# A two-layer GLA/NSA trunk: three weight chunks of layer 0 land in tiles of later tenants, the second output projection uses other banks, gates are written in place

## Chip, core and metric

The kernel runs on one core of a Trainium2 chip, as one program. The metric is the device time of one execution in microseconds (us). Five engines work in parallel, each through its own list of instructions in order: TensorE (PE, matmuls, with its weight loads as PEld), VectorE (DVE), ScalarE (ACT), GpSimd (POOL) and SyncE (SP), which issues nearly all loads here. They wait for one another by semaphores.

## What is computed

A trunk of two layers over 256 tokens of width 1024, all float32. Each layer is `x + rms_norm(mixer(rms_norm(x)))`. The mixer of layer 0 is chunked gated linear attention (GLA), that of layer 1 is native sparse attention (NSA). Cut to its core:

```python
def gla_mixer(h, w_in, w_gk_up, b_gk, head_norm, w_out):
    p = h @ w_in
    q, k, v, glr, z = jnp.split(p, [512, 1024, 2048, 2064], axis=-1)
    gk = jax.nn.log_sigmoid(glr @ w_gk_up + b_gk) / 16.0
    o = gla_chunked(heads(q, 128) * 128 ** -0.5, heads(k, 128), heads(v, 256), heads(gk, 128))
    o = rms_norm(o, head_norm)
    return (o * jax.nn.silu(z)) @ w_out

def nsa_mixer(h, ...):
    q, kc, vc, ks, vs, kw, vw, gl, z = jnp.split(h @ w_in, splits, axis=-1)
    # rope; compressed, selected and sliding-window softmax attention, gated by sigmoid(gl)
    return (gated_sum * jax.nn.silu(z)) @ w_out

def reference(x, ...):
    for i in range(2):
        h = rms_norm(x, pre_norm[i])
        y = gla_mixer(h, ...) if i == 0 else nsa_mixer(h, ...)
        x = x + rms_norm(y, post_norm[i])
    return x
```

## The kernel before

The 256 tokens are two tiles of 128, called t = 0 and t = 1. All products are made from split operands: a float32 value is written as hi (rounded by ACT's copy) plus lo (the rest, a subtraction on DVE or POOL), and `mm3` (L211 to L213) adds three matmuls, hi·hi, hi·lo and lo·hi, into one PSUM bank. `hT` is the normalized input, transposed and split.

Weights come in **chunks** of up to 512 columns. A `Chunk` has four units of 256 rows; `load` issues one DMA a unit from SP into a raw tile, `split_unit` makes two hi's on ACT (L190) and two lo's (L196) by a unit, on POOL or DVE by the table `LOS`. In layer 0 the chunks are, in order: r (the last columns of v and the decay's input glr), k, q, v0, v1 (344 columns each), z0, z1 (512 each), and then the two halves of the output weights. Chunks r, k and q have a written-out order on each engine (`split_in_line`, L434 and L438, with `line("act", ...)` and the like); the later ones are ordered by the tile scheduler, by explicit orders (`after`, `chain` for PE, `prev`) and by `paced`, which ties a split to a matmul of an earlier chunk. In layer 1 the chunks are kc, ks, kw, q, z and the output weights.

What is scarce sets the order of much of this:

- Raw tiles: four tiles of tag "raw" are shared by all chunks. A load waits until the lo's of the unit that had the tile before are done. SP's queue is in order, so a load that waits holds all behind it. One chunk, k, lands elsewhere: two units in `home`, a tile in the place that zT takes later, and one each in the places of "on" and "gpost", which also come later.
- PSUM banks: two of tag "acc", three "s", two "t", one "o". `proj` (v and the chunks of layer 1 with rows out) takes one "acc" bank for each t; `proj_T` (q and z, transposed) two. A bank is free when its evacuation is done: L517 on ACT and L518 on DVE for v, L363 for z, L618 for q, L269 on ACT and L276 on DVE for an output projection.
- The buffer of tag "of", a single one: it holds z (the bank times `rb`, the tokens' norm factors) while the tanh (L371, ACT) and the product (L372, DVE) make the gate in zT; `gated` (L356 to L358: DVE, ACT, DVE) uses the same tag.

Around the v chunks, `decay(t)` computes the log-sigmoid on ACT and DVE (L598 to L606), L633 multiplies it with a triangular matrix on PE, L636 and L637 take exponentials on ACT, and L644, L650, L661 and L662 scale q and k with them on DVE. `out_proj(t)` runs 16 steps of `mm3` over the 8 row blocks k and the two halves n of the output, the first four k first, since the gates of the second z chunk come late; then `residual` reads the banks (L269, L276), scales and adds to X (L281), and `pre_T` transposes the new X (L302 on PE) into hT of layer 1 (L307, L310, L311). That of t = 1 runs beside the first chunk of layer 1, kc, whose half for t = 0 needs only the tokens of t = 0.

The lines which set these places:

```python
o = [bank("s" if t == 0 else "acc") for _ in range(2)]            # out_proj
z = base.tile([P, 2, S], F32, tag="of", name=nm("z"))             # gate_of
ch_k = Chunk(w_in, G_K, 512).load(homes=[home[:, 0], home[:, 1], "on", "gpost"])
ch_v0 = Chunk(w_in, 1024, 344).load()
simple(ch_v0, lambda o, t: to_v(o, t, 0, 344), (ch_q, PA[1]), prev=queues["act"])
```

Of the kernel before, what the change touches and what calls it, by code (L numbers as in the profile page):

```python
# [16 lines left out]
P = 128  # L17
# [70 lines left out]
def hybrid_kernel(ctx: ExitStack, tc: tile.TileContext, x, positions, pre_norm, post_norm,  # L88
# [9 lines left out]
    def nm(s):  # L98
        _n[0] += 1
        return f"{s}_{_n[0]}"  # L100
# [54 lines left out]
    grow = lp.tile([2 * KT, P], F32, tag="grow", name="grow")  # L155
    nc.scalar.dma_start(X[:, 0, :H], xv[:, 0, :H])
    nc.scalar.dma_start(grow, pre_norm.rearrange("l (k p) -> (l k) p", p=P))
    dma(C0, cst[:, :C_L0])
    dma(X[:, 1, :H], xv[:, 1, :H])

# [179 lines left out]
    def out_proj(t, chunks, oT, gb):  # L340

        o = [bank("s" if t == 0 else "acc") for _ in range(2)]
        steps = [(k, n) for k in range(4) for n in range(2)] + [(k, n) for n in range(2) for k in range(4, KT)]
        done = residual(t, o, gb)
        for k, n in steps:
            a, b = mm3(o[n], [h[:, k, :] for h in oT[t]], chunks[n].part(k), k == 0, k == KT - 1)
            first = a if k == n == 0 else first
            if k == KT - 1:
                done(n)
        chain(first, b)  # L350

    def gated(bv, zt, hi, lo):

        of = base.tile([P, 4, P], F32, tag="of", name=nm("of"), bufs=1)
        of = of[:, :bv.shape[1], :]
        nc.vector.tensor_mul(of, bv, zt)  # L356
        nc.scalar.activation(hi, of, AF.Copy)
        return nc.vector.tensor_sub(lo, of, f(hi))  # L358

    def gate_of(o, dst):  # L360

        z = base.tile([P, 2, S], F32, tag="of", name=nm("z"))
        nc.vector.tensor_tensor(z, o.rearrange("p (j n) -> p j n", j=2), rb.unsqueeze(1).to_broadcast([P, 2, S]),  # L363
                                op=ALU.mult)
        silu2(z, dst)

    tanh = [None]

    def silu2(o, dst):

        tanh[0] = after(nc.scalar.activation(dst, o, AF.Tanh, scale=0.5), tanh[0])  # L371
        nc.vector.scalar_tensor_tensor(dst, dst, 1.0, o, op0=ALU.add, op1=ALU.mult)  # L372

# [7 lines left out]
    home = lp.tile([P, 2, 2, 512], F32, tag="zT", name="home")  # L381
    ch_k = Chunk(w_in, G_K, 512).load(homes=[home[:, 0], home[:, 1], "on", "gpost"])
    wraw = lp.tile([32, 512], F32, tag="E", name="wraw")
# [138 lines left out]
    def from_r(t):  # L522
# [12 lines left out]
        line("act", a)  # L535
        line("dve", b)
        glrs.append(glr)

    split_in_line(ch_k, 0)
# [3 lines left out]
    split_in_line(ch_k, 2)  # L543
    for t in range(NT):
        from_r(t)
    split_in_line(ch_k, 3)

# [9 lines left out]
    line("pool", nc.gpsimd.tensor_copy(wup[64:64 + n], f(wup[:n])))  # L557
    for u in range(4):
        split_in_line(ch_q, u)
# [55 lines left out]

    ch_v0 = Chunk(w_in, 1024, 344).load()
    for j, o in enumerate(proj_T(ch_q, hT, dict(zip(GM, (gates_T, lambda: decay(0), lambda: decay(1)))))):
# [4 lines left out]
    scale = float(np.float32(GDK ** -0.5))  # L622
    zT = lp.tile([P, KT, S], F32, tag="zT", name="zT")
    aTs, qees, kdds = [], [], []
# [52 lines left out]

    simple(ch_v0, lambda o, t: to_v(o, t, 0, 344), (ch_q, PA[1]), prev=queues["act"])
    ch_z = [Chunk(w_in, G_Z, 512).load()]
    simple(ch_v1, lambda o, t: to_v(o, t, 344, 688), (ch_v0, PA[2]))  # L680
    ch_z.append(Chunk(w_in, G_Z + 512, 512).load())
    gpost = row(post_norm, 0, D, lp, "gpost")

# [34 lines left out]
    for c in range(2):  # L718
        ch_z[c].split(((ch_v1, PA[3]), (ch_z[0], PA[4]))[c])
        for j, o in enumerate(proj_T(ch_z[c], hT)):  # L720
# [524 lines left out]
```

## Time and profile before

| | |
|---|---|
| median of 3 runs | 311.4 us (310.65 to 311.85) |
| the profiled execution | 312.61 us |
| its span in the profile | 310.5 us |
| granted TensorE clock, mean | 0.979 |
| busy: PE, DVE, ACT, POOL | 289.7, 217.3, 180.8, 167.7 us |
| DMA queue of SP | 43.96 MB, 45.2% of 16 engines' span |

A row of the timeline gives start and duration in us, the engine, the line of the kernel, the operation with the names of what it writes and reads, shapes, and a count where equal instructions that follow each other are joined; in brackets stands how long the engine was idle before it and what ended that. The list of waits groups such brackets. The granted clock is the share of its full rate that TensorE was given in a stretch. A stretch of PE's timeline tells more than its busy share over the span: at 93% it is one wait at a time that can still go.

### The profile page before, as it was taken

To read this page: it belongs to the slowest core of one execution; us is meant where nothing else is said; L and a number is where in the kernel's file an instruction comes from. 1 tells how busy PE (TensorE), PEld (TensorE's weight loads), DVE (VectorE), ACT (ScalarE), POOL (GpSimd) and SP (SyncE) were. 2 spreads that over 40 slices of the span, in tenths; PEclk is the share of its full clock that TensorE was granted. 3 is DMA by queue.
4 is the path that set the end of the run, shared out by engine and by line. 5 is a ranking of instruction groups with operands and counts; after the bars stand their busy time and mean duration, and the time that the engine had idled before them with its cause. 6 is when DMAs were issued, how large, how long until landed. Compare 5 with 4: busy or idle time off the path is not lost.

```text
span 310.5 us, 5351 instructions
## 1 busy us (share of the span) xinstructions
PE 289.7 (93%) x1788; PEld 242.3 (78%) x1788; DVE 217.3 (70%) x556; ACT 180.8 (58%) x468; POOL 167.7 (54%) x184
## 2 busy tenths in 40 slices
PE   6999989989999899499997999999999989999991
PEld 6888978989999688377895866789878877677551
DVE  0677847665888778766588452879997899696523
ACT  3786586878476259524453430657986569565211
POOL 1294719988449106652544512599758974533400
PEclk9999997999999999689999999999999999999998
DMA  7990504868737505485265568657602600010001
GB/s 226 395 309 1 155 30 129 256 204 268 241 103 229 179 0 153 146 199 183 76 179 167 155 251 271 218 162 235 201 2 72 199 1 2 2 69 0 2 0 68
DMA packets 28300, 44.56 MB, mean 144 GB/s; under 512 B 2865, under 2 KB 12513, under 8 KB 28274
## 3 DMA queue, kind: packets, MB, share of 16 engines
q1 hardware_dynamic: 28098, 43.96, 45.2%
q10 hardware_dynamic: 176, 0.27, 0.3%
q8 instruction: 14, 0.23, 0.3%
q14 instruction: 12, 0.10, 0.1%
HBM read 43.18 MB, written 1.05 MB: 142 GB/s over the span
## 4 chain that ended last, share of the span: by engine, by line
PE 61%; DVE 17%; issue 9%; DMA 4%; POOL 4%; ACT 3%; SPq 0%; POOLq 0%; DVEq 0%; ACTq 0%
PE acc L211 12%; PE acc L213 11%; PE acc L212 11%; DVE lo L196 6%; PE s L466 4%; PE o L1078 3%; PE o L884 3%; PE s L991 3%; DMA raw<-in_gla_w_in_dram 3%; PE t L1064 3%; PE s L211 3%; PE s L212 2%; PE s L213 2%; POOL lo L196 2%; DMA raw<-in_nsa_w_out_dram 1%
## 5 line engine op out<-in xcount | busy, mean ns | idle before, releaser
L196 POOL TENSOR_TENSOR lo<-raw,hi 128x512 fp32r<-128x512 f32 (+2 forms) x69 | 89.5, 1321 | 44.5 <-ACT hi L190 43.3
L190 ACT ACTIVATE hi<-raw 128x512 fp32r<-128x512 f32 (+2 forms) x128 | 68.2, 580 | 38.3 <-DMA raw<-in_nsa_w_in_dram 21.0
L196 DVE TENSOR_TENSOR lo<-raw,hi 128x512 fp32r<-128x512 f32 (+2 forms) x59 | 54.6, 946 | 19.0 <-ACT hi L190 18.9
L211 PE MATMUL acc<-hi,hT 128*128 128x512 f32 (+2 forms) x112 | 41.0, 366 | 5.1 <-DVE yg L276 4.0
L211 PE MATMUL acc<-hT,hi 128*128 128x256 f32 x160 | 45.1, 283 | 0.1
L213 PE MATMUL acc<-hT,lo 128*128 128x256 f32 x160 | 44.6, 282 | 0.0
L212 PE MATMUL acc<-hT,hi 128*128 128x256 f32 x160 | 44.5, 279 | 0.0
L1035 POOL TENSOR_SCALAR P<-P,cf 128x128 f32<-128x128 f32 (+1 forms) x64 | 29.9, 488 | 26.0 <-DVE cf L1031 14.3
L212 PE MATMUL acc<-lo,hT 128*128 128x512 f32 (+2 forms) x112 | 40.7, 363 | 1.0 <-POOL lo L196 0.7
L213 PE MATMUL acc<-hi,hT 128*128 128x512 f32 (+2 forms) x112 | 39.9, 356 | 0.0
L998 ACT ACTIVATE P<-P,mn 128x128 f32<-128x128 f32 (+1 forms) x64 | 28.4, 445 | 8.9 <-DVE mn L996 5.1
L211 PEld LDWEIGHTS acc<-hT,hi 128*128 128x128 f32 x160 | 30.0, 188 | 0.3 <-DVE z L363 0.3
L213 PEld LDWEIGHTS acc<-hT,lo 128*128 128x128 f32 x160 | 29.8, 188 | 0.5 <-issue 0.4
L212 PEld LDWEIGHTS acc<-hT,hi 128*128 128x128 f32 x160 | 30.1, 188 | 0.1
L211 PEld LDWEIGHTS acc<-hi,hT 128*128 128x128 f32 x112 | 22.0, 197 | 9.8 <-ACT hi L190 5.4
L212 PEld LDWEIGHTS acc<-lo,hT 128*128 128x128 f32 x112 | 22.0, 196 | 3.9 <-POOL lo L196 1.8
L996 DVE CUSTOM_DVE_ANT_0 P<-s,c 128x128 f32<-128x128 f32 (+1 forms) x64 | 20.7, 348 | 4.9 <-PE s L991 3.7
L213 PEld LDWEIGHTS acc<-hi,hT 128*128 128x128 f32 x112 | 22.0, 196 | 2.7 <-issue 0.4
L438 POOL TENSOR_TENSOR lo<-raw,hi 128x512 fp32r<-128x512 f32 (+1 forms) x9 | 11.6, 1302 | 14.7 <-ACT hi L434 14.7
L1064 PE MATMUL t<-c,P 128*128 128x128 f32 x96 | 16.6, 284 | 0.4 <-DVE qS L959 0.4
L275 POOL TENSOR_TENSOR ss<-ss,cols 128x1 f32<-128x1 f32 x4 | 2.2, 552 | 26.3 <-DVE ss L274 26.3
L822 POOL TENSOR_TENSOR dup<-rt,rt 128x512 f32<-128x512 f32 x6 | 8.6, 1438 | 13.4 <-DVE rt L815 11.3
(265 smaller groups left out, 675.0 us busy)
## 6 DMA issues: line engine op xcount, KB each, us to landing
raw<-in_nsa_w_in_dram SPq DMA_DIRECT2D x24, 512.0 KB, 4.5
raw<-in_gla_w_in_dram SPq DMA_DIRECT2D x14, 512.0 KB, 4.6
raw<-in_gla_w_out_dram SPq DMA_DIRECT2D x8, 512.0 KB, 5.0
raw<-in_nsa_w_out_dram SPq DMA_DIRECT2D x8, 512.0 KB, 4.3
raw<-in_gla_w_in_dram SPq DMA_DIRECT2D x8, 344.0 KB, 3.5
raw<-in_nsa_w_in_dram SPq DMA_DIRECT2D x8, 280.0 KB, 7.9
w<-in_nsa_ck_w_dram SPq DMA_DIRECT2D x4, 512.0 KB, 3.7
w<-in_nsa_cv_w_dram SPq DMA_DIRECT2D x4, 512.0 KB, 4.7
```

The costliest lines, as they stand in the source:

```text
L190: m = after(nc.scalar.activation(hi[:, j, :n], raw[:, j, :n], AF.Copy), prev)
L196: eng.tensor_sub(lo[:, j, :n], raw[:, j, :n], f(hi[:, j, :n]))
L211: m = nc.tensor.matmul(o, a[0], b[0], start=start, stop=False, **kw)
L212: nc.tensor.matmul(o, a[0], b[1], start=False, stop=False, **kw)
L213: return m, nc.tensor.matmul(o, a[1], b[0], start=False, stop=stop, **kw)
L438: line(e, eng.tensor_sub(lo[:, j, :n], raw[:, j, :n], f(hi[:, j, :n])))
L466: m = nc.tensor.matmul(o[t][:, :chunk.n], hT[i][:, k, t * P:(t + 1) * P], w[j], start=(k == b == 0), stop=(k == KT - 1 and b == 2))
L884: nc.tensor.matmul(hid_b[kv * 64:(kv + 1) * 64, :CHID], flat[:, j, kv].rearrange("p g c -> p (g c)"), w1[u * 2 + kv][:, j % 4, :], start=( ...
L996: nc.vector.tensor_tensor_reduce(out=o, in0=src, in1=masks[br], op0=ALU.add, op1=ALU.min, scale=-0.125, scalar=3.0e38, accum_out=self.mn[: ...
L998: nc.scalar.activation(o, o, AF.Exp, scale=-1.0, bias=self.mn[:, j:j + 1], accum_out=self.sm[:, j:j + 1])
L1035: nc.gpsimd.tensor_scalar(o, o, cf[:, i * 2 + br:i * 2 + br + 1], 1.0, op0=ALU.mult, op1=ALU.mult)
L1064: pe(nc.tensor.transpose(b[:, i * P:(i + 1) * P], self.Pt[i][:, c0:c0 + P], ident))
```

## The change

1. The head: the first half of X for t = 0 is loaded from SP's queue, behind the constants, and no longer first on ACT's queue.
2. `out_proj(1)` takes one "s" and one "acc" bank; before, it took two "acc". `out_proj(0)` keeps two "s".
3. `gate_of` writes the product with `rb` straight into its place in zT; the tanh goes to a tile of tag "xg", and the product is made in zT. `gated` takes its buffer from "xg" too. Of "xg" there are two, which the residual's yg and pre_T's products use as well. These functions serve both layers.
4. The homes are used by three chunks in turn: k, v0 and z0. zT is allocated only after z0 is split.
5. In the written-out order, the hi's of k's fourth unit go ahead of `from_r` and its lo's ahead of that function's DVE halves (now returned to the caller), and q's first unit is split ahead of the decay's transposes.
6. The splits of v0 are no longer ordered behind the end of ACT's written-out list (`prev`), only paced by q's matmuls.

```diff
-    nc.scalar.dma_start(X[:, 0, :H], xv[:, 0, :H])
     nc.scalar.dma_start(grow, pre_norm.rearrange("l (k p) -> (l k) p", p=P))
     dma(C0, cst[:, :C_L0])
-    dma(X[:, 1, :H], xv[:, 1, :H])
+    for t in range(NT):
+        dma(X[:, t, :H], xv[:, t, :H])
...
-        o = [bank("s" if t == 0 else "acc") for _ in range(2)]
+        o = [bank("s"), bank("acc" if t else "s")]
...
-        of = base.tile([P, 4, P], F32, tag="of", name=nm("of"), bufs=1)
+        of = base.tile([P, 4, P], F32, tag="xg", name=nm("of"), bufs=2)
...
-        z = base.tile([P, 2, S], F32, tag="of", name=nm("z"))
-        nc.vector.tensor_tensor(z, o.rearrange("p (j n) -> p j n", j=2), rb.unsqueeze(1).to_broadcast([P, 2, S]),
+        nc.vector.tensor_tensor(dst, o.rearrange("p (j n) -> p j n", j=2), rb.unsqueeze(1).to_broadcast([P, 2, S]),
                                 op=ALU.mult)
-        silu2(z, dst)
+        th = base.tile([P, 2, S], F32, tag="xg", name=nm("th"), bufs=2)
+        silu2(dst, dst, th)
...
-    def silu2(o, dst):
-        tanh[0] = after(nc.scalar.activation(dst, o, AF.Tanh, scale=0.5), tanh[0])
-        nc.vector.scalar_tensor_tensor(dst, dst, 1.0, o, op0=ALU.add, op1=ALU.mult)
+    def silu2(o, dst, th=None):
+        th = dst if th is None else th
+        tanh[0] = after(nc.scalar.activation(th, o, AF.Tanh, scale=0.5), tanh[0])
+        nc.vector.scalar_tensor_tensor(dst, th, 1.0, o, op0=ALU.add, op1=ALU.mult)
...
-    ch_k = Chunk(w_in, G_K, 512).load(homes=[home[:, 0], home[:, 1], "on", "gpost"])
+    homes = [home[:, 0], home[:, 1], "on", "gpost"]
+    ch_k = Chunk(w_in, G_K, 512).load(homes=homes)
...
-    for t in range(NT):
-        from_r(t)
-    split_in_line(ch_k, 3)
+    w = hi_of(ch_k, 3)
+    for j in range(2):
+        w[0](j)
+    rest = [from_r(t) for t in range(NT)]
+    for j in range(2):
+        w[1](j)
+    for b in rest:
+        line("dve", b)
+    split_in_line(ch_q, 0)
...
-    for u in range(4):
+    for u in range(1, 4):
         split_in_line(ch_q, u)
...
-    ch_v0 = Chunk(w_in, 1024, 344).load()
+    ch_v0 = Chunk(w_in, 1024, 344).load(homes=homes)
...
-    zT = lp.tile([P, KT, S], F32, tag="zT", name="zT")
...
-    simple(ch_v0, lambda o, t: to_v(o, t, 0, 344), (ch_q, PA[1]), prev=queues["act"])
-    ch_z = [Chunk(w_in, G_Z, 512).load()]
+    simple(ch_v0, lambda o, t: to_v(o, t, 0, 344), (ch_q, PA[1]))
+    ch_z = [Chunk(w_in, G_Z, 512).load(homes=homes)]
     simple(ch_v1, lambda o, t: to_v(o, t, 344, 688), (ch_v0, PA[2]))
     ch_z.append(Chunk(w_in, G_Z + 512, 512).load())
+    ch_z[0].split((ch_v1, PA[3]))
+    zT = lp.tile([P, KT, S], F32, tag="zT", name="zT")
...
-        ch_z[c].split(((ch_v1, PA[3]), (ch_z[0], PA[4]))[c])
+        if c:
+            ch_z[1].split((ch_z[0], PA[4]))
```

The changed kernel is longer, so its line numbers run 2 to 10 higher behind the middle of layer 0: L598 becomes L606, L434 becomes L436, L363 becomes L362.

The first place is ACT at the decay chain of layer 0. Before, the decay of t = 1 (tmp, gk) and the exponentials of t = 0 (E, En) stand there, and v0's eight hi's follow, from raw tiles:

```order
L598 ACTIVATE tmp_493<-t_491 128x512
L599 ACTIVATE tmp_493<-tmp_493 128x512
L600 ACTIVATE tmp_493<-tmp_493 128x512
L636 ACTIVATE E_559<-t_561 128x2x192
L637 ACTIVATE En_560<-t_561 128x256
L602 ACTIVATE gk_358<-tmp_493 128x512
L190 ACTIVATE hi_666<-raw_416 128x344 x2
L190 ACTIVATE hi_672<-raw_418 128x344 x2
L190 ACTIVATE hi_678<-raw_420 128x344 x2
L190 ACTIVATE hi_684<-raw_422 128x344 x2
```

In the changed program they follow q's last unit (hi_348), and the decay of t = 0 comes behind them:

```order
L436 ACTIVATE hi_348<-raw_110 128x512 x2
L190 ACTIVATE hi_663<-home 128x344 x2
L190 ACTIVATE hi_669<-home 128x344 x2
L190 ACTIVATE hi_675<-raw_418 128x344 x2
L190 ACTIVATE hi_681<-raw_420 128x344 x2
L606 ACTIVATE tmp_456<-t_454 128x512
L607 ACTIVATE tmp_456<-tmp_456 128x512
```

v0's hi's moved ahead of the whole decay chain. The names raw_418 and raw_420 are its third and fourth unit, which lie in the places of "on" and "gpost".

The second place is DVE at the gates of layer 0's second z chunk; acc_1113 and acc_1114 (before), acc_1109 and acc_1110 (now) are the two banks of that projection, and lo_1316 and lo_1312 belong to the output weights:

```order
L363 TENSOR_TENSOR z_1211<-acc_1113,rb 128x512
L196 TENSOR_TENSOR lo_1316<-raw_1313,hi_1315 128x512
L372 SCALAR_TENSOR_TENSOR zT<-zT,z_1211 128x512
L363 TENSOR_TENSOR z_1215<-acc_1114,rb 128x512
L372 SCALAR_TENSOR_TENSOR zT<-zT,z_1215 128x512
```

```order
L362 TENSOR_TENSOR zT<-acc_1109,rb 128x512
L362 TENSOR_TENSOR zT<-acc_1110,rb 128x512
L196 TENSOR_TENSOR lo_1312<-raw_1309,hi_1311 128x512
L373 SCALAR_TENSOR_TENSOR zT<-th_1208,zT 128x512
L373 SCALAR_TENSOR_TENSOR zT<-th_1212,zT 128x512
```

The two evacuations moved together, ahead of both products. The gates of layer 1 changed in the same way.

The third place is ACT around the second output projection and the first chunks of layer 1. Before; hi_1551 to hi_1569 are ks's units, L269 reads the two banks of out_proj(1), and dup_1628 evacuates kc's half for t = 0:

```order
L190 ACTIVATE hi_1551<-raw_1543 128x512 x2
L190 ACTIVATE hi_1557<-raw_1545 128x512 x2
L269 ACTIVATE yg_1426,ss_1425<-acc_1423 128x512
L269 ACTIVATE yg_1427,ss_1425<-acc_1424 128x512
L190 ACTIVATE hi_1563<-raw_1547 128x512 x2
L190 ACTIVATE hi_1569<-raw_1549 128x512 x2
```

and now:

```order
L190 ACTIVATE hi_1547<-raw_1539 128x512 x2
L190 ACTIVATE hi_1553<-raw_1541 128x512 x2
L190 ACTIVATE hi_1559<-raw_1543 128x512 x2
L190 ACTIVATE hi_1565<-raw_1545 128x512 x2
L269 ACTIVATE yg_1422,ss_1421<-s_1419 128x512
L269 ACTIVATE yg_1423,ss_1421<-acc_1420 128x512
```

All of ks's hi's moved ahead of the reading of the banks. On PE, the transposes of the new X for t = 1 (L302) moved too. Before, they stood nine matmuls ahead of the end of ks's half for t = 0 (acc_1651):

```order
L213 MATMUL acc_1651<-hi_1563,hT_1322 128x512
L302 MATMUL t_1485<-c_64,x_sb 128x128 x4
L302 MATMUL t_1494<-c_64,x_sb 128x128 x4
L211 MATMUL acc_1651<-hi_1563,hT_1321 128x512
L212 MATMUL acc_1651<-lo_1564,hT_1321 128x512
```

Now they stand behind it (acc_1647), ahead of kc's half for t = 1 (acc_1698):

```order
L213 MATMUL acc_1647<-hi_1565,hT_1318 128x512
L302 MATMUL t_1481<-c_64,x_sb 128x128 x4
L302 MATMUL t_1490<-c_64,x_sb 128x128 x4
L815 MATMUL t_1596<-c_64,vecs 128x32
L211 MATMUL acc_1698<-hi_1515,hT_1317 128x512
```

The nine matmuls of ks that stood behind the transposes moved ahead of them.

More of the change, by code (lines that the diff above doesn't have):

```diff
@@ L535, in from_r @@
         line("act", a)
-        line("dve", b)
         glrs.append(glr)
+        return b
     split_in_line(ch_k, 0)
```

## Prediction

> **What bounds the kernel now.** I read the page's busy times first, then the list of what PE waited for, then PE's timeline around each wait, and last the granted clock there.
>
> ```profile
> PE 289.7 (93%) x1788; PEld 242.3 (78%) x1788; DVE 217.3 (70%) x556; ACT 180.8 (58%) x468; POOL 167.7 (54%) x184
> ```
>
> PE is busy for 289.7 of 310.5 us. The matmuls are the same before and after, so only PE's idle time and the time at a lower clock can change: some 21 us idle, and what the clock costs. The first and last few us are not touched; what the change can reach are single waits:
>
> ```profile
> PE acc L211 <- DVE yg L276: 4.0, 1, 4.0
> PE o L483 <- DMA grow<-in_pre_norm_dram: 1.8, 1, 1.8
> PE o L884 <- DVE flat L875: 1.6, 1, 1.6
> PE acc L211 <- DVE z L363: 1.3, 1, 1.3
> ```
>
> Each of these is one event. The clock has its own price. Columns: the stretch, its length, busy time (x instructions) of PE, PEld, DVE, ACT and POOL, granted clock, DMA:
>
> ```profile
> 44.87:48.28 3.41, 2.28 (x9) 1.10 (x7) 1.31 (x2) 3.41 (x11) 2.85 (x4) 1.00 0.00 0
> 48.28:51.69 3.41, 3.41 (x14) 3.35 (x15) 3.41 (x4) 1.27 (x4) 3.41 (x3) 0.53 0.69 189
> 123.37:126.79 3.42, 1.12 (x5) 0.58 (x4) 3.42 (x8) 2.91 (x8) 0.78 (x1) 1.00 0.89 247
> 126.79:130.20 3.41, 1.72 (x4) 1.46 (x5) 3.27 (x6) 1.98 (x4) 2.96 (x3) 0.53 0.18 66
> 130.20:133.61 3.41, 3.41 (x9) 2.64 (x9) 0.05 (x1) 0.00 (x0) 3.41 (x4) 0.50 0.51 126
> 164.33:167.75 3.42, 1.82 (x19) 1.21 (x20) 3.39 (x10) 1.15 (x2) 0.85 (x1) 1.00 0.72 219
> ```
>
> The clock is about half in two places, each right behind a stretch with few matmuls (9 and 5). The stretch with the 1.6 us wait at 164 had 19 and kept a clock of 1.00. So a wait of 1 to 1.6 us costs no clock here while matmuls stand around it.
>
> **The change, part by part. A, the v projections** (layer 0, 43 to 69 us).
>
> ```profile
> 43.02 0.63 PE L633 MATMUL t<-ct,gk 128*128 128x256 f32 x4
> 46.52 0.42 PE L212 MATMUL acc<-lo,hT 128*128 128x344 f32 x1 [0.69 <-POOL lo L196]
> 64.47 0.43 PE L211 MATMUL acc<-hi,hT 128*128 128x344 f32 x1 [0.88 <-DVE v L518]
> 68.64 0.32 PE L213 MATMUL acc<-hi,hT 128*128 128x344 f32 x1
> 68.80 0.28 PE L211 MATMUL acc<-hT,hi 128*128 128x256 f32 x1
> ```
>
> From 43.02 to the first z matmul at 68.80 are 25.78 us. In it stand 96 v matmuls, 0.16 apart when they run freely (68.64 to 68.80): 15.4. Sixteen of L633 at 0.63 for four are 2.5; two wide ones of L641 and the small ones of L659, L666 and L668 I estimate at 2.5 from the same row. That makes 20.4, so 5.4 us are lost. Why:
>
> ```profile
> 36.13 0.97 POOL L573 CAST ct<-c 128x384 fp32r<-128x384 f32 x1
> 45.43 7.50 POOL L196 TENSOR_TENSOR lo<-raw,hi 128x344 fp32r<-128x344 f32 x7 [8.34 <-ACT hi L190]
> 44.86 3.14 ACT L190 ACTIVATE hi<-raw 128x344 fp32r<-128x344 f32 x8
> 47.38 5.95 SPq L125 DMA_DIRECT2D raw<-in_gla_w_in_dram  x4
> raw<-in_gla_w_in_dram SPq DMA_DIRECT2D x8, 344.0 KB, 3.5
> ```
>
> POOL stood idle for 8.34 us because v0's hi copies came after the decay chain on ACT. Then its seven lo's take 1.07 each, slower than PE eats them; PE runs thin, and the clock halves for the 3.41 us (1.6 us of the loss). v1's loads are issued as v0's lo's free the raw tiles (47.38 on) and land 3.5 us later. In the new program v0 lands in the homes of k, its hi's stand ahead of the decay chain, and v1's loads wait only for the tiles of q. POOL is free at 37.1, so seven lo's end at about 44.7, when PE has just begun with them at 43.7. What is new is that POOL goes on with v1's lo's, and that DVE runs these operations beside it:
>
> ```profile
> 49.86 1.40 DVE L644 TENSOR_TENSOR kdd<-kdd,k_sb 128x512 f32<-128x512 f32 x1
> 51.18 0.68 DVE L661 TENSOR_TENSOR ke<-t,En 128x512 f32<-128x512 f32 x1
> ```
>
> Of two equal operations under POOL's seven lo's, the one with two SBUF inputs took 1.40, the one that reads a bank 0.68. In the new order DVE has five of the first kind (three v1 lo's, qe, kdd) between gk and v's evacuation: 7.0 us from 45.7, so that evacuation (0.56) ends near 53.3, about when PE, after 48 matmuls and the small ones, wants its bank; the second half's, behind five more operations, has no more slack. I charge 0.8 for one such wait, the nearest being the 0.88 above, and 0.5 for starts like the row at 46.52. **A: 5.4 - 1.3 = 4.1 gained.** If each of the five waited out a whole POOL lo of 1.07 and then took 0.68, it would be 1.75 instead of 1.40, 1.8 us in all, and A 2.3; that is a rival below. The Trainium skill's page "SBUF — State Buffer", section "Who interferes with whom", says that a DVE instruction with two SBUF inputs contends with a GpSimd instruction that reads SBUF, and that the loser blocks until the other is done. The two rows agree in direction; whether a whole lo is waited out they don't show. The ends of A are 5.4 (no wait) and 2.3.
>
> **B, the gates of z1 before the output projection** (104 to 107).
>
> ```profile
> 106.96 0.50 PE L211 MATMUL s<-hi,oT 128*128 128x512 f32 x1 [0.96 <-ACT oT L357]
> 102.66 0.68 DVE L372 SCALAR_TENSOR_TENSOR zT<-zT,z 128x512 f32<-128x512 f32 x1
> 103.37 0.69 DVE L363 TENSOR_TENSOR z<-acc,rb 128x512 f32<-128x512 f32 x1
> 104.10 0.63 ACT L371 ACTIVATE zT<-z 128x512 f32<-128x512 f32 x1 [1.92 <-DVE z L363]
> ```
>
> The second z could be evacuated only when the one buffer had gone through its tanh and product; that chain ends in oT at 106.9. Now both evacuations stand side by side, one tanh time (0.6) and one product (0.7) earlier, and PE has the first twelve matmuls of out_proj(1)'s acc bank (0.22 each, 2.7 us) to run before it needs that oT. The 0.96 and the slow first step go. **B: 1.1** (0.5 to 1.4).
>
> **C, from out_proj(1) to layer 1's first chunk** (119 to 134).
>
> ```profile
> 119.34 1.03 PE L302 MATMUL t<-c,x_sb 128*128 128x128 f32 x8
> 123.88 0.39 PE L212 MATMUL acc<-lo,oT 128*128 128x512 f32 x1
> 124.10 0.39 PE L213 MATMUL acc<-hi,oT 128*128 128x512 f32 x1
> 128.48 0.77 PE L211 MATMUL acc<-hi,hT 128*128 128x512 f32 x1 [3.99 <-DVE yg L276]
> 133.31 0.63 PE L213 MATMUL acc<-hi,hT 128*128 128x512 f32 x1
> 125.02 0.58 ACT L269 ACTIVATE yg<-acc 128x512 f32<-128x512 f32 x1
> 128.44 1.15 ACT L190 ACTIVATE hi<-raw 128x512 fp32r<-128x512 f32 x2 [0.82 <-DMA raw<-in_nsa_w_in_dram]
> 125.19 2.48 DVE L196 TENSOR_TENSOR lo<-raw,hi 128x512 fp32r<-128x512 f32 x4
> 127.66 1.27 DVE L276 SCALAR_TENSOR_TENSOR yg<-acc,gpost 128x512 f32<-128x512 f32 x2
> ```
>
> Both acc banks belonged to out_proj(1); kc's first matmul waited for L276, 3.99 us, and the clock halved: 12 matmuls to 133.31 stand 0.44 apart instead of 0.22, 2.4 us more. Together 6.4. With one bank "s", kc0 (kc's half for t = 0) takes the free acc bank and starts at once. **What is late next** is ks0, 24 matmuls (5.4 us) on: it needs the acc bank that out_proj(1) kept, and L269 now stands behind all eight ks hi's on ACT, L276 behind four lo's on DVE. If the last ks load were as late as in the row (128.44), L269 twice (2 x 0.6) would end at 130.8 and the second L276 at 131.4 at the latest, against kc0's end at 124.3 + 5.4 = 129.7: a wait of 1.7, or 2.1 with the accumulator reads. The loads come earlier, as kc's lo's now stand ahead of the residual; at best the wait is 0. I take 1.1. Then the transposes of t = 1 (L302) come where no matmul of ks0 is left; before, nine followed (2.0 us) and covered their evacuation:
>
> ```profile
> 123.66 1.28 DVE L311 TENSOR_TENSOR hT<-xg,hT 128x512 fp32r<-128x512 f32 x2
> ```
>
> One evacuation of 0.6, one hi on ACT and the first half of L311 are some 1.3 to 1.8 us; I take 1.3. **C: 6.4 - 1.1 - 1.3 = 4.0.** Ends: 6.3 if neither wait comes, and 6.4 - 2.1 - 1.7 - 1.7 = 0.9 if both come in full and one 3.41 us stretch at half clock with them.
>
> The Trainium skill, "TensorE: Matmul & The Clock Gate", "Why this matters for your kernels", asks for no PE gap over about 3 us. The row at 44.87 speaks against that as the only condition, since the clock fell with no gap over 0.69. By the page ks0's stall could not halve the clock, and C's low end would be 2.6; I go by the rows and keep 0.9.
>
> **Z, the gates of layer 1** (248). gate_of is used there too.
>
> ```profile
> 247.56 1.22 DVE L372 SCALAR_TENSOR_TENSOR zT<-zT,z 128x512 f32<-128x512 f32 x1
> 248.82 0.68 DVE L363 TENSOR_TENSOR z<-acc,rb 128x512 f32<-128x512 f32 x1
> ```
>
> The second z waited behind the first's product (L372), and PE 1.28 for it (1.3 in the list). Both evacuations now stand ahead of both products. **Z: 1.2** (0.5 to 1.4).
>
> **The rest.** Head: X's first half moves from ACT's queue to SP's behind C0; grow starts one issue earlier, and PE waits for grow (1.8). I take 0, between a gain of 0.2 and a loss of 0.4. The flat wait (1.6) has the same order around it: 0. Layer 0's z chunks and the attention are reordered around unchanged matmuls, and waits like the 0.88 and 0.69 above can appear anew, once in each: **1.4 lost**, between nothing and 4.
>
> Sum: 4.1 + 1.1 + 4.0 + 1.2 - 1.4 = **9.0 us gained**. The profiled execution took 312.6 (span 310.5 and 2.1 around it), so 303.6; it lies 1.2 over the median of the runs, 311.4, so **302.5**.
>
> **Rivals.** (1) *The stall moves to ks0 whole*: C gives 0.9 in place of 4.0, and the time is 305.6. For it: ACT's order. Against: earlier loads. Chance 0.18. (2) *Few new waits*: A 5.4, B 1.1, C 5.1 (ks0 in time, hT(1) not), Z 1.2, nothing elsewhere: 12.8, so 298.6. Against it: every wait that goes has a successor in sight. Chance 0.14. (3) *DVE blocked by POOL in A*: 1.8 us less, 304.3; the page on SBUF would have it so. For it: 1.40 beside 0.68. Chance 0.10. (4) *The change doesn't do what it says in A*, v's waits being POOL's rate and not the raw tiles: A nil, and with (1) 5.9 - 4.1 = 1.8 less 0.5 of new waits: 310.1, within 0.5% of before. Against it: the 8.34 us in which POOL stood idle. Chance 0.07. (5) *Slower: the attention loses its filler.* Place: 208 to 226 us.
>
> ```profile
> 207.90:226.00 18.10, 16.96 (x139) 16.02 (x137) 17.75 (x81) 14.91 (x52) 15.58 (x23) 1.00 0.68 204
> ```
>
> There DVE is busy 17.75 of 18.10 and PE's idle share is small only because z matmuls fill in. If the last z chunk is used up earlier, PE has to wait for DVE's softmax rows. Each z matmul moved away from such a stretch costs up to 0.12 (68.80's kind of 256 columns), a chunk of 96 up to 11 us. It decides from 88 matmuls on (9.0 + 1.6 us over 0.12): then 313 or more. Against it: the z rows moved by ten to twenty places, not by a chunk. Chance 0.06. The forecast itself: 0.45.
>
> About 0.5%, 1.6 us, is what a measurement of this kernel can tell from no change. Forecast and (1) to (3) are faster: 0.87; (4) is within: 0.07; (5) slower: 0.06. The range 298.0 to 308.5 leaves out (4), (5) and the far ends of (2) and of the unknown 4 us elsewhere.
>
> **What would show it.** Right: no wait of kc on L276, but one of about 1 us at ks0; no half clock at 48 and at 127 to 134; POOL's lo's of v0 before 45; no wait on z in either layer. Wrong: half clock behind ks0, v0 still waiting for lo's, or new waits of several us in the attention.

## The result, and the profile after the change

The changed kernel takes 302.79 us (median of 4 runs, 302.69 to 303.20) against 311.21 (310.65 to 311.85) before: a ratio of 0.9731, with a 95% interval of 0.9709 to 0.9753. Its profiled execution took 302.72 with a span of 300.8. The forecast was 302.5. Executions of one and the same kernel differ in their mean granted clock and with it in time: those of the kernel before show 0.979 to 0.993 and 310.6 to 313.5 us, and its profiled one lies at the low end of the clock.

The first view is the page's busy times and the granted clock by slice, then the list of what PE waited for (us in total, times, longest):

```profile
PE 286.6 (95%) x1788; PEld 239.7 (80%) x1788; DVE 215.3 (72%) x556; ACT 181.5 (60%) x468; POOL 167.0 (56%) x184
PEclk9999999999999999999999999999997799999998
```

```profile
PE t L1074 <- ACT pcT L1096: 1.9, 2, 1.8
PE o L894 <- DVE flat L885: 1.6, 1, 1.6
...
PE acc L211 <- DVE yg L276: 0.8, 1, 0.8
PE t L815 <- DVE xg L307: 0.7, 1, 0.7
PE t L415 <- DMA x_sb<-in_x_dram: 0.6, 1, 0.6
PE acc L211 <- ACT hT L310: 0.4, 1, 0.4
```

Of the four waits that the prediction quoted, three are gone: kc's 4.0, the head's 1.8 on grow, and 1.3 on z. The wait on flat stands as it did. One new wait leads the list, in the attention of layer 1 (pcT holds the transposed weights of the compressed keys), and the two slices with the lowest clock (7) lie there.

To see where the time went, the start of the first matmul of each stage was read from PE's timeline, in every kernel alike. Each figure below is the length of one stage in us; the last five columns are experiments that are told further down, the last of them one of the two fastest kernels here. kw is the third chunk of layer 1, behind kc and ks.

| stage, from first matmul to first matmul | before | after | head alone | homes alone | banks alone | gates alone | old gates in layer 1 |
|---|---|---|---|---|---|---|---|
| start of span to q | 30.88 | 29.27 | 29.30 | 30.38 | 30.12 | 30.34 | 29.40 |
| q to v | 14.53 | 12.47 | 14.51 | 12.47 | 14.54 | 14.51 | 12.47 |
| v to z | 23.40 | 18.94 | 23.46 | 18.95 | 23.36 | 23.38 | 18.94 |
| z to out_proj | 31.46 | 31.93 | 31.54 | 31.94 | 31.20 | 31.20 | 31.93 |
| out_proj to kc | 28.21 | 23.03 | 28.21 | 27.95 | 23.49 | 27.43 | 23.03 |
| kc to kw | 27.43 | 27.80 | 26.54 | 26.95 | 27.80 | 27.38 | 27.80 |
| that to layer 1's z | 51.79 | 51.62 | 51.63 | 51.75 | 52.53 | 51.64 | 51.69 |
| layer 1's z to layer 1's output projection | 39.19 | 41.62 | 39.18 | 39.01 | 39.19 | 41.53 | 39.19 |
| that to the start of the last matmul | 56.99 | 57.46 | 56.98 | 57.19 | 57.00 | 57.80 | 56.97 |

From before to after that is 1.6 gained at the head, 6.5 in the two v stages, 5.2 from out_proj to kc, and 2.4 lost in layer 1's attention; the rest is below 0.5 each.

**The v projections.** The stretch before and after (length, busy time (x instructions) of PE, PEld, DVE, ACT and POOL, clock, DMA):

```profile
45.41:68.80 23.39, 21.44 (x128) 19.71 (x129) 16.70 (x21) 17.57 (x39) 22.65 (x19) 0.93 0.58 179
```

```profile
41.74:60.68 18.94, 18.94 (x133) 18.64 (x131) 16.02 (x20) 14.98 (x34) 16.04 (x13) 1.00 0.60 189
```

PE is now busy for the whole stage. POOL's timeline shows why; lo<-home are v0's first two units:

```profile
33.36 0.79 POOL L581 CAST ct<-c 128x384 fp32r<-128x384 f32 x1
34.11 3.59 POOL L196 TENSOR_TENSOR lo<-home,hi 128x344 fp32r<-128x344 f32 x4
37.67 3.15 POOL L196 TENSOR_TENSOR lo<-raw,hi 128x344 fp32r<-128x344 f32 x3
```

The 8.34 us in which POOL stood idle are gone; the first seven lo's end at 40.8, before v begins at 41.74, where before they began at 45.43.

**The first chunks of layer 1**, from PE's timeline:

```profile
115.64 0.50 PE L211 MATMUL acc<-hi,hT 128*128 128x512 f32 x1
...
122.51 0.47 PE L211 MATMUL acc<-hi,hT 128*128 128x512 f32 x1 [0.76 <-DVE yg L276]
...
129.94 0.24 PE L815 MATMUL t<-c,vecs 32*128 32x32 f32 x1 [0.71 <-DVE xg L307]
130.60 0.50 PE L211 MATMUL acc<-hi,hT 128*128 128x512 f32 x1 [0.42 <-ACT hT L310]
```

kc begins with no wait. What is late next is ks's first half (0.76), then the transposes of t = 1 (0.71 and 0.42).

**The attention of layer 1.** Ahead of the last few us the granted clock falls to half once, behind a stretch with 13 matmuls, which holds the 1.8 us wait on pcT:

```profile
226.28:229.69 3.41, 1.85 (x13) 0.88 (x11) 3.35 (x15) 2.10 (x8) 3.41 (x6) 1.00 0.73 244
229.69:233.10 3.41, 3.10 (x12) 1.94 (x12) 3.41 (x11) 3.15 (x13) 3.41 (x4) 0.50 0.01 2
233.10:236.52 3.42, 3.42 (x15) 2.45 (x14) 3.42 (x13) 0.94 (x3) 0.70 (x3) 0.50 0.00 0
```

### The profile page after: what moved, and what is told of

Its sections match the earlier page's. It is cut to its first block, busy times and chain, and to the rows that moved or that the text cites. A ratio compares the mean times of both kernels' runs of the same rounds, so it can differ in the third digit from the quotient of the medians.

```text
span 300.8 us, 5374 instructions
## 1 busy us (share of the span) xinstructions
PE 286.6 (95%) x1788; PEld 239.7 (80%) x1788; DVE 215.3 (72%) x556; ACT 181.5 (60%) x468; POOL 167.0 (56%) x184
## 4 chain that ended last, share of the span: by engine, by line
PE 63%; DVE 13%; issue 9%; POOL 6%; ACT 4%; DMA 3%; SPq 0%; POOLq 0%; DVEq 0%; ACTq 0%
PE acc L211 11%; PE acc L213 11%; PE acc L212 11%; PE s L468 4%; POOL lo L196 3%; PE s L212 3%; PE s L211 3%; PE s L213 3%; DVE lo L196 3%; PE o L894 3%; PE t L1074 3%; PE o L1088 3%; PE s L1001 2%; ACT hi L190 2%; DMA raw<-in_gla_w_in_dram 1%
## 5 line engine op out<-in xcount | busy, mean ns | idle before, releaser
L196 POOL TENSOR_TENSOR lo<-raw,hi 128x512 fp32r<-128x512 f32 (+2 forms) x63 | 82.8, 1334 | 44.4 <-ACT hi L190 44.4
L190 ACT ACTIVATE hi<-raw 128x512 fp32r<-128x512 f32 (+2 forms) x120 | 64.2, 583 | 37.7 <-DMA raw<-in_nsa_w_in_dram 26.6
L196 DVE TENSOR_TENSOR lo<-raw,hi 128x512 fp32r<-128x512 f32 (+2 forms) x57 | 53.6, 963 | 13.4 <-ACT hi L190 13.3
L211 PE MATMUL acc<-hi,hT 128*128 128x512 f32 (+2 forms) x112 | 39.2, 350 | 1.2 <-DVE yg L276 0.8
L213 PE MATMUL acc<-hi,hT 128*128 128x512 f32 (+2 forms) x112 | 38.9, 347 | 0.0
L212 PE MATMUL acc<-lo,hT 128*128 128x512 f32 (+2 forms) x112 | 38.8, 346 | 0.0
L211 PEld LDWEIGHTS acc<-hi,hT 128*128 128x128 f32 x112 | 21.1, 188 | 5.3 <-ACT yg L269 1.2
L213 PEld LDWEIGHTS acc<-hi,hT 128*128 128x128 f32 x112 | 21.1, 188 | 2.9 <-DVE hT L311 0.4
L212 PEld LDWEIGHTS acc<-lo,hT 128*128 128x128 f32 x112 | 21.1, 188 | 2.0
L1074 PE MATMUL t<-c,P 128*128 128x128 f32 x96 | 17.4, 296 | 2.0 <-ACT pcT L1096 1.9
L440 POOL TENSOR_TENSOR lo<-raw,hi 128x512 fp32r<-128x512 f32 (+1 forms) x9 | 12.3, 1388 | 9.9 <-ACT hi L436 9.8
L1074 PEld LDWEIGHTS t<-c,P 128*128 128x128 f32 x96 | 11.1, 147 | 7.3 <-issue 3.6
```

The costliest lines, as they stand in the source:

```text
L190: m = after(nc.scalar.activation(hi[:, j, :n], raw[:, j, :n], AF.Copy), prev)
L196: eng.tensor_sub(lo[:, j, :n], raw[:, j, :n], f(hi[:, j, :n]))
L211: m = nc.tensor.matmul(o, a[0], b[0], start=start, stop=False, **kw)
L212: nc.tensor.matmul(o, a[0], b[1], start=False, stop=False, **kw)
L213: return m, nc.tensor.matmul(o, a[1], b[0], start=False, stop=stop, **kw)
L440: line(e, eng.tensor_sub(lo[:, j, :n], raw[:, j, :n], f(hi[:, j, :n])))
```

## The experiments

Ratios are to the kernel before, timed alongside, with 95% intervals.

**One part at a time.** The change has four parts that can be made alone. The head:

```diff
-    nc.scalar.dma_start(X[:, 0, :H], xv[:, 0, :H])
-    dma(X[:, 1, :H], xv[:, 1, :H])
+    for t in range(NT):
+        dma(X[:, t, :H], xv[:, t, :H])
```

> The kernel before with the first part alone: X's first half from SP's queue, grow first on ACT's. Theory: the 1.17 us by which the changed kernel's first transposes start earlier (4.28 against 5.45) come from grow landing sooner, and every engine behind keeps them: 311.2 - 1.2 = 310.0, PE's wait on grow gone. Rival, the forecast's step: nothing, 311.2, C0 or X being as late as grow was.

Measured: 309.67 us, 0.9932 [0.9911, 0.9954]. The head, held at 0, is worth something: 1.6 us in the table against the one profile of before, about 1.0 against the three other kernels with the old head. PE's wait on grow is gone. The rest of the 2.1 us lies far behind it, in kc's stage (26.54 for 27.43): the wait of 3.99 us is as long as before, but the clock then stays halved for one stretch of 3.41 us, not two, which need not be the head's doing (see the last section).

The homes of v0 and of z0, with the splits that go with them (the changed kernel with the other three parts as before):

```diff
-    for t in range(NT):
-        dma(X[:, t, :H], xv[:, t, :H])
+    nc.scalar.dma_start(X[:, 0, :H], xv[:, 0, :H])
+    dma(X[:, 1, :H], xv[:, 1, :H])
...
-        o = [bank("s"), bank("acc" if t else "s")]
+        o = [bank("s" if t == 0 else "acc") for _ in range(2)]
...
+        z = base.tile([P, 2, S], F32, tag="of", name=nm("z"))
...
```

> The kernel before with the homes for v0 and z0, the new order of k's and q's splits and v0's free splits; the head, the banks and the gates as before. Theory: this carries the whole gain of the v stretch as the changed kernel shows it, 6.4 us (L633 to the first z matmul 19.4 instead of 25.8), less 0.5 in the stretch behind: 305.3. Rival, the forecast's size: 4.1, so 307.1. If the gain needs the earlier head, 309 or more.

Measured: 305.07, 0.9789 [0.9764, 0.9814], and the two v stages as in the changed kernel (12.47 and 18.95). The whole of A's gain belongs to this part.

The banks:

```diff
-        o = [bank("s" if t == 0 else "acc") for _ in range(2)]
+        o = [bank("s"), bank("acc" if t else "s")]
```

> The kernel before with the second output projection in one s and one acc bank, nothing else. Theory: the 3.99 us wait of kc on L276 and the half clock behind it go, a wait of about 1 at ks0 and about 1.2 at the second kc half come, and the twelve matmuls that can run early cover the z1 wait of 0.96: 311.2 - 3.6 - 1.0 = 306.6. Rival: the stall moves to ks0 whole, 310.

Measured: 307.62, 0.9854 [0.9830, 0.9879], a gain of 4.2 where the theory had 4.6 and the rival 1.2. Out_proj to kc is 4.7 shorter, 4.0 of it kc's wait. This also shows where most of B's gain comes from: the stage takes 23.49 here with the old gates, 23.03 in the changed kernel.

The gates (z evacuated into its place in zT, the tanh's buffer and gated's in two buffers of the tag "xg"):

```diff
-        z = base.tile([P, 2, S], F32, tag="of", name=nm("z"))
-        nc.vector.tensor_tensor(z, o.rearrange(...
+        nc.vector.tensor_tensor(dst, o.rearrange(...
...
-        silu2(z, dst)
+        th = base.tile([P, 2, S], F32, tag="xg", name=nm("th"), bufs=2)
+        silu2(dst, dst, th)
```

> The kernel before with the gates in place and two buffers in both layers, nothing else. Theory: layer 0's z wait goes (1.0), but in layer 1 the order of the attention changes as in the changed kernel, with PE waiting about 1.8 us for pcT and 6.8 us at half clock, 2.9 lost there net of the z wait of 1.28: 311.2 - 1.0 + 2.9 = 313.1, slower. Rival, the forecast's step: both z waits go and nothing comes, 311.2 - 2.3 = 308.9.

Measured: 314.18, 1.0082 [1.0054, 1.0110]. Made alone, this part makes the kernel slower. What PE waited for here:

```profile
PE acc L211 <- ACT yg L269: 4.5, 1, 4.5
PE t L1065 <- ACT pcT L1087: 2.0, 2, 1.8
```

The wait on z is gone, and the same wait on pcT has come as in the changed kernel; layer 1's z stage is 41.53 for 39.19. The four parts alone add up to 10.5 us (2.1 + 6.7 + 4.2 - 2.4) where all together give 8.4: the banks and the gates remove the same microsecond ahead of out_proj, and the head and the banks the same half clock behind kc's wait.

**Layer 1's gates undone.** The changed kernel, with the old gates (z and of in one buffer of the tag "of") in layer 1 only:

```diff
-                gate_of(o[j], zT[:, p * 4 + j * 2:p * 4 + j * 2 + 2, :])
+                gate_of1(o[j], zT[:, p * 4 + j * 2:p * 4 + j * 2 + 2, :])
...
-            gated(self.ob.rearrange("p (i n) -> p i n", i=2), zT[:, sl, t * P:(t + 1) * P],
+            gated1(self.ob.rearrange("p (i n) -> p i n", i=2), zT[:, sl, t * P:(t + 1) * P],
```

> The changed kernel with the gates of layer 1 made as before (one buffer of tag of for z and for gated), those of layer 0 in place; from the attention on every engine's order is the one of before. Theory: the gates in place lose layer 1 what the changed kernel lost there (from the first z matmul to the last matmul 99.1 us instead of 96.2), so 302.8 - 2.9 = 299.9, with the wait of PE on z (1.3) back and those on pcT (1.8) and the half clock at 230 gone. Rival: the loss came from the earlier arrival of layer 1, not from the gates: 302.8, or 304 with the z wait added.

Measured: 300.2 (299.81 to 301.54), 0.9638 [0.9605, 0.9671]: faster than the changed kernel by more than the intervals, and as fast as any here. PE waits 1.3 on z again, and the stage is 39.19 long all the same. The stage is cut here at the last z matmul; first the changed kernel, then this one:

```profile
195.06:225.74 30.68, 30.58 (x250) 28.86 (x249) 29.57 (x111) 25.77 (x80) 27.13 (x35) 1.00 0.49 156
225.74:236.68 10.94, 9.06 (x45) 5.88 (x43) 10.85 (x37) 6.71 (x22) 8.22 (x11) 0.69 0.28 94
```

```profile
195.25:231.42 36.17, 35.02 (x280) 31.89 (x279) 32.90 (x133) 29.17 (x94) 29.73 (x43) 1.00 0.43 132
231.42:234.44 3.02, 3.02 (x24) 2.20 (x23) 2.92 (x6) 0.61 (x3) 3.02 (x2) 1.00 0.77 229
```

With z in place, the 192 z matmuls are through 5.5 us earlier, and what they ran beside comes behind them with no filler (matmuls that PE can run while others wait): 10.94 us, with idle time and a clock of 0.69, where the old gates leave 3.02.

The same with the old gates in both layers (`gated`, `gate_of` and `silu2` as before):

> The changed kernel with the gates made as before in both layers. Theory: in layer 0 the twelve matmuls that out_proj(1) can run early cover the wait on oT (0.96) without the gates, as the kernel with the banks alone shows no such wait; so the same as with the old gates in layer 1 alone within 0.3: 299.9. Rival: the z chunk's gates in layer 0 are worth their 1.0: 300.9.

Measured: 300.2, 0.9628 [0.9593, 0.9662]. In layer 0 the gates in place are worth nothing that can be seen once the banks are changed (out_proj to kc 23.20, with them 23.03).

**What makes A.** The wait for the end of ACT's queue put back, with v0 still in the homes:

```diff
-    simple(ch_v0, lambda o, t: to_v(o, t, 0, 344), (ch_q, PA[1]))
+    simple(ch_v0, lambda o, t: to_v(o, t, 0, 344), (ch_q, PA[1]), prev=queues["act"])
```

> The changed kernel with v0's splits ordered behind ACT's written-out list again, the homes kept. Theory: the free splits carry most of the v gain, since POOL's lo's (about 1.05 each, 7 of 8) start at 43 instead of 34 and set the pace of v0 again; only v1's earlier loads stay: about 4 of the 6.4 are lost, 306.5. Rival: the raw tiles were the limit and the homes alone suffice: 303.

Measured: 309.47, 0.9932 [0.9904, 0.9960], so much slower than either expectation. POOL's timeline:

```profile
44.34 3.96 POOL L196 TENSOR_TENSOR lo<-home,hi 128x344 fp32r<-128x344 f32 x4 [9.82 <-ACT hi L190]
```

POOL stands idle as in the kernel before, for 9.82 us, and the v stage takes 22.50. Two more us are lost at q to v (14.39), and 3.0 from layer 1's output projection to the last matmul (60.43 for 57.46). In this execution (311.15 us, 1.7 over the median) the half clock lies there:

```profile
241.86:248.69 6.83, 6.83 (x24) 4.63 (x23) 4.34 (x23) 4.44 (x16) 3.27 (x8) 0.50 0.02 4
```

The output projection starts at 241.96, and PE is busy throughout, so half the clock over 6.83 us costs up to 3.4 (an estimate from this row). In the changed kernel the same length at half clock ends at 236.52, just ahead of the projection at 236.68.

And the reverse: the splits free, but v0 in raw tiles:

```diff
-    ch_v0 = Chunk(w_in, 1024, 344).load(homes=homes)
+    ch_v0 = Chunk(w_in, 1024, 344).load()
```

> The changed kernel with v0 in raw tiles again (k and z0 keep the homes), its splits free. Theory: the free splits need the homes: v0's loads wait for q's lo's again, its hi's then stand on ACT in front of the decay chain and wait for them, and v1's loads wait for v0's lo's: 2 to 3 us of the v gain lost, 305.3. Rival: order alone is what matters: 302.8.

Measured: 307.12, 0.9851 [0.9829, 0.9874]. ACT's timeline:

```profile
33.57 0.87 ACT L190 ACTIVATE hi<-raw 128x344 fp32r<-128x344 f32 x2 [2.24 <-DMA raw<-in_gla_w_in_dram]
```

The hi's now wait for their loads, but early enough: the v stage takes 20.33, 1.4 more than with the home. Another 2.7 are lost from out_proj to kc (25.77), where PE waits 1.55 for hT ahead of kc. So in the two v stages the free splits are the larger part of A (5.5 us lost without them), and the home of v0 the smaller (1.4).

**The new wait of C.** The kernel with layer 1's old gates, and the third and fourth ks units held behind the residual's last Square on ACT:

```diff
-    ch_ks.split()
+    ch_ks.split_unit()
+    ch_ks.split_unit(sq[0])
+    ch_ks.split_unit(sq[0])
...
-            nc.scalar.activation(yg[n], o[n], AF.Square, accum_out=ss[:, n:n + 1])
+            sq[0] = nc.scalar.activation(yg[n], o[n], AF.Square, accum_out=ss[:, n:n + 1])
```

> As e5 (old gates in layer 1), and on ACT the two reads of out_proj(1)'s banks (L269) go ahead of the third and fourth unit of ks's hi's. Theory: the wait at ks0 (0.76, with its slow start 0.9) comes from ACT's order alone and goes; ks's later lo's are still in time: 0.9 under e5, 299.0. Rival: DVE's four lo's ahead of L276 hold the bank just as long, or ks's third unit is late instead: the same as e5.

Measured: 300.59, 0.9650 [0.9615, 0.9684], the same as without the edit. ks's wait is gone (kc's stage 26.96 for 27.80), but the gain doesn't reach the end: layer 1's z stage is 40.22 for 39.19, the 1.03 more all behind the start of its last z matmul (4.14 for 3.11), where PE now waits 0.86 for DVE's evacuation of z. DVE's timeline there, first without the edit, then with it:

```profile
229.53 0.71 DVE L373 TENSOR_TENSOR ofT<-of,ofT 128x256 fp32r<-128x256 f32 x1 [0.60 <-ACT ofT L372]
230.99 0.96 DVE L196 TENSOR_TENSOR lo<-raw,hi 128x512 fp32r<-128x512 f32 x1 [0.30 <-ACT hi L190]
```

```profile
228.97 1.33 DVE L375 TENSOR_TENSOR ofT<-of,ofT 128x256 fp32r<-128x256 f32 x1 [1.26 <-ACT ofT L374]
230.68 1.32 DVE L196 TENSOR_TENSOR lo<-raw,hi 128x512 fp32r<-128x512 f32 x1
```

DVE runs the same instructions in the same order, beside POOL's lo's in both kernels, and yet ofT took 1.33 us for 0.71 and lo 1.32 for 0.96. Counted from the span's start they begin up to 0.6 us earlier with the edit, and end at about the same time. What differs is when they start inside a lo of POOL's. POOL's rows, first without the edit, then with it:

```profile
228.66 1.30 POOL L196 TENSOR_TENSOR lo<-raw,hi 128x512 fp32r<-128x512 f32 x1
```

```profile
228.73 1.29 POOL L196 TENSOR_TENSOR lo<-raw,hi 128x512 fp32r<-128x512 f32 x1
```

These end at 229.96 and 230.02, and ofT ends 0.28 behind each; DVE's lo ends 0.55 behind the next of POOL's (231.40 and 231.44) in both. So DVE waited out POOL's lo both times, and starting earlier only made the wait longer.

**Which half of layer 1's gates costs.** z in place, but `gated` in its own buffer (the old `gated1`, the new `gate_of`):

> The changed kernel, but in layer 1 gated has a buffer of its own (tag of, one) again; the gates stay in place with two tanh tiles. On PE the last z matmul again stands behind 11 of layer 1's products of q and k, as in the changed kernel (13 before). Theory: it is the early evacuation of z that moves the filler, so the loss stays: 302.8. Rival: the shared buffers hold ACT and DVE up: 300.

Measured: 306.2, 0.9826 [0.9804, 0.9848], 3.4 slower than the changed kernel and slower than either expectation; the z stage takes 44.13. And the reverse, the old z with `gated` in the two shared buffers (`gate_of1`, the new `gated`):

> The changed kernel, but in layer 1 z has the one buffer of before, and gated uses the two shared buffers. The last z matmul stands behind 13 products of q and k, as before. Theory: filler in its old place, no loss: 300.2. Rival, the shared buffers: 302.8.

Measured: 301.94, 0.9689 [0.9672, 0.9707]; the z stage 39.43, and 1.7 more behind it (58.65 for the 56.97 with all old gates). Of the two, it is z in place that costs in this stage. The shared buffers cost less, and behind it.

**Filler later.** The changed kernel, with the second z chunk written between the parts of the unit behind it:

```diff
-    run(z_steps(1))
-    unit(3, 0)
+    zs = z_steps(1)
+    run(zs, 4)
+    run(U[3, 0].scores())
+    run(zs, 2)
+    v3 = U[3, 0].values()
+    run(v3, 2)
+    run(zs)
+    run(v3)
```

> The changed kernel with the last z chunk of layer 1 written later: four row blocks, then the scores of unit (3,0), two more row blocks, two steps of that unit's values, the last two. The last z matmul stands behind 14 products of q and k instead of 11. Theory: with z matmuls left around the first transposes of the last units PE has work while it waits for pcT, the wait of 1.8 and the half clock at 230 go: 300.0. Rival: pcT is late for ACT's order (hi's that wait for loads ahead of it) and DVE's, and more products stand between the last z matmul and the output projection (19 instead of 17): 302.8 or slower.

Measured: 303.01, 0.9732 [0.9693, 0.9770], no gain. But the edit did little of what it was for:

```profile
194.85:226.31 31.46, 31.36 (x256) 29.62 (x255) 30.31 (x119) 27.30 (x88) 27.91 (x36) 1.00 0.55 167
226.31:237.51 11.20, 6.96 (x45) 4.13 (x43) 11.10 (x39) 7.38 (x25) 8.63 (x12) 0.92 0.14 50
```

Only six more matmuls stand among z's (256 for 250), and the stretch without filler is as long as before. PE's wait on pcT is gone, but waits on DVE came in its place, the longest of them

```profile
PE o L1088 <- DVE pT L1080: 2.3, 1, 2.3
```

and DVE is busy for 11.10 of these 11.20 us. This profiled execution, 306.06, lies 3 us over the median and has 10.24 us at half clock; four of the six took 301.85 to 303.29 at a mean clock of 0.987 to 0.995, where the changed kernel's four have 0.984. So the half clock can go and the time falls by 0.9 at most. The run neither shows nor refutes that a later filler would mend the stage.

## Why the prediction was right, and where its steps were not

The total was 0.3 us off, partly by luck: B and C came out within 0.4, the head and A 1.6 and 2.4 too low, and layer 1's attention with the rest some 3 too high. (The prediction's own terms add up to 302.4.)

- **Head: the step failed.** It said "grow starts one issue earlier" and took 0. grow did not merely start earlier: from issue to landing it took 4.0 us before, behind X's half in ACT's queue, and 1.9 after. X's first transposes on PE start at 4.28 us for 5.45; the head alone is worth 1.0 to 1.6. The ten kernels with the new head reach q at 28.93 to 29.93 us, the four with the old one at 30.12 to 30.88.
- **A: right mechanism, term mis-sized** (4.1 forecast, 6.5 measured over the two v stages). POOL's idle time went as forecast. From the first four matmuls of L640 (L633 before) to the first z matmul it now takes 19.41 us (41.27 to 60.68), where the estimate without losses was 20.4 and 1.3 of new waits were charged on top. Neither wait came, and PE has no gap in the stage. The five DVE operations ahead of v's evacuation were priced at 1.40 each, 7.0 us; they took 4.94:

```profile
43.86 1.68 DVE L196 TENSOR_TENSOR lo<-raw,hi 128x344 fp32r<-128x344 f32 x2
46.25 0.69 DVE L657 SCALAR_TENSOR_TENSOR qe<-qT,E 128x512 f32<-128x512 f32 x1 [0.71 <-ACT E L643]
46.96 1.15 DVE L196 TENSOR_TENSOR lo<-raw,hi 128x344 fp32r<-128x344 f32 x1
48.03 1.42 DVE L651 TENSOR_TENSOR kdd<-kdd,k_sb 128x512 f32<-128x512 f32 x1
49.38 0.56 DVE L520 SCALAR_TENSOR_TENSOR v<-acc,rs_r,v 128x344 fp32r<-128x344 f32 x1
```

- **A's share of the clock was wrong.** "1.6 us of the loss" was put down to the half clock behind the thin stretch. With the banks alone the clock stays at 1.00 there, and the stage is as long (23.35 for the 23.39 of the row of before):

```profile
44.66:68.01 23.35, 20.65 (x128) 18.25 (x129) 17.61 (x21) 17.61 (x39) 22.56 (x19) 1.00 0.59 181
```

  POOL's lo's set the pace at 22.56 of 23.35 us busy, and PE at half clock only idled less.
- **B: right in size, its cause only in part.** 1.2 came (1.1 forecast: out_proj to kc without kc's wait of 3.99 is 24.22 before, 23.03 after), but the banks alone bring 0.7 of it (23.49), and with the head and the homes changed too the gates add only 0.17 in layer 0 (23.20 to 23.03).
- **C: held.** 3.6 for 4.0 (5.2 from out_proj to kc, less B's 1.2 and the 0.4 by which kc's stage grew): kc's wait and the half clock are gone, the wait at ks is 0.76 (1.1 forecast), the two at hT 0.71 and 0.42 (1.3 forecast). Rival (1), the whole stall at ks, did not come.
- **Z and "the rest" in the attention: the step failed.** PE's wait on z went as forecast, and the stage became 2.4 us longer where +1.2 was expected of it. The prediction took the wait as the price. But while z stood in that one buffer, its wait also spaced the z matmuls; without it they were done 5.5 us earlier. This looks like rival (5)'s mechanism, the attention losing its filler, at a smaller size: 36 z matmuls (those that the kernel with old gates starts later than 30.57 us into its stage, where the changed one starts its last) moved out of the softmax, and 2.4 us lost is 0.07 for each, a little over half of the 0.12 that was its upper price. Each of the six kernels with z in place has its last z matmul start 30.5 to 31.4 us into the stage and a stage of 41.1 to 44.1 us; the others 35.9 to 38.3 and 39.0 to 40.2. That z in place costs is shown by undoing it; that the missing filler is how is read from these traces, and the one edit meant to test it moved too little. PE's one long wait there is for ACT's queue:

```profile
227.78 1.15 ACT L190 ACTIVATE hi<-raw 128x512 fp32r<-128x512 f32 x2 [1.31 <-DMA raw<-in_nsa_w_out_dram]
228.84 0.39 ACT L1008 ACTIVATE P<-P,mn 128x128 f32<-128x128 f32 x1
...
229.61 0.25 ACT L1096 ACTIVATE pcT<-t 64x128 f32<-64x128 f32 x1
```

  pcT's evacuation stands behind two hi's that wait 1.31 for a load and behind softmax rows. In the kernel with old gates, two hi's wait 2.03 for such a load and pcT comes at 229.40; PE has z matmuls to run meanwhile.

  A rival that no run separates from the missing filler is DVE's own pace. In the changed kernel DVE is busy for 40.4 of the stage's 41.6 us, and for 10.85 of the 10.94 without filler; with old gates for 35.8 of 39.2. Thirteen small operations of the attention (cf, the branches' factors, and cS, the scores of the compressed keys) take 7.7 us in the changed kernel and 3.8 with old gates; six of them, in place of two, run beside one of POOL's lo's and take 0.5 us or more:

```profile
222.78 1.39 DVE L1055 TENSOR_TENSOR cS<-cS,cm 128x64 f32<-128x64 f32 x1
222.81 1.28 POOL L196 TENSOR_TENSOR lo<-raw,hi 128x512 fp32r<-128x512 f32 x1
```

```profile
220.90 0.20 DVE L1070 TENSOR_TENSOR cS<-cS,cm 128x64 f32<-128x64 f32 x1
```

  The first two rows are the changed kernel, the third the one with old gates, where POOL is idle at that moment. Z in place moved the lo's and the softmax against each other as well as the filler.

Of the other rivals, (2) came nearest on the v stages (A 5.4 for 6.5) and had the attention wrong; (3) fell by its size, not by its mechanism: of the five operations none took 1.75 and qe only 0.69. (4) fell with the two experiments on A, which show that late hi's and not POOL's rate alone held v up. The Trainium skill's "SBUF — State Buffer", "Who interferes with whom", has the loser block until the other is done, and the traces agree. kdd, at 48.03 in the rows of A, starts inside this lo of POOL's:

```profile
47.70 1.21 POOL L196 TENSOR_TENSOR lo<-raw,hi 128x344 fp32r<-128x344 f32 x1
```

It ends at 49.45, 0.55 behind the end of that lo; so do kdd and qe of before (1.40 and 1.41 us) and gk of the changed kernel (1.39), within 0.01. What is waited out is the rest of the lo in which the operation starts, not a whole one on top: qe started 0.08 before the end of a lo and took 0.69. In layer 1's z stage the cS of 1.39 above starts with a lo and ends at 224.17, 0.08 behind it, and each of the six such cf and cS ends within 0.1 us of the end of a lo.

## What to carry to other kernels

Price a stretch from its two ends in the trace and from what would set its pace next, not by adding the waits inside it: here the sum of waits missed A by 2.4 us, and Z with the rest by 3. A wait on a shared buffer may be what spaces an engine's filler; before it is removed, ask what that filler will stop covering. And make each part of a change alone once: here the change without its gates in layer 1, or without them at all, is best: 300.2 us, 0.964 and 0.963 of before.

## What the runs showed of the hardware that was not expected

- The clock fell to half behind 13 matmuls in 3.41 us with one gap of 1.79, and not behind 19 with a gap of 1.6 (the row at 164 of before). Nor did it in the changed kernel behind 14 with a gap of 1.57 and the same busy time, 1.84 us for 1.85:

```profile
151.19:154.60 3.41, 1.84 (x14) 0.96 (x14) 3.38 (x10) 1.43 (x3) 0.18 (x1) 1.00 0.79 258
154.60:158.01 3.41, 3.41 (x30) 2.66 (x27) 2.68 (x6) 1.30 (x3) 3.41 (x3) 1.00 0.02 5
```

  The Trainium skill ("TensorE: Matmul & The Clock Gate", "Why this matters for your kernels") warns of PE gaps over about 3 us; here the clock fell with none that long.
- The same wait of 3.99 us halved the clock for two stretches (6.83 us) before and for one (3.41) with the head alone, worth 0.9 us. The v stage halved the clock in two kernels (before, head alone) and left it whole in two with the same waits (banks, gates alone). It isn't the kernel alone: executions of the kernel before have mean clocks of 0.979 to 0.993, and by an estimate one stretch of 3.41 us at half clock takes 0.0055 off that mean (half of 3.41 over 310.5), so their number changes from one execution to the next. What decides is open.
- The same two-input DVE operation, gk, took 1.39 us beside POOL's lo's, ending 0.55 behind the lo in which it started, and 0.69 with POOL idle:

```profile
37.75 1.39 DVE L614 TENSOR_TENSOR gk<-tmp,gk 128x512 fp32r<-128x512 f32 x1 [0.70 <-ACT gk L610]
...
43.25 0.69 DVE L614 TENSOR_TENSOR gk<-tmp,gk 128x512 fp32r<-128x512 f32 x1 [0.60 <-ACT gk L610]
```
